# Both recurrent mixers of a streaming encoder layer on full 128x128 products, with the sample's tokens in a zero-padded third chunk

## The chip, the core and the metric

The program runs on one core of one Trainium2 chip. The metric is the device time of one execution in microseconds (us). The core has a tensor engine (PE; its weight loads are shown apart as PEld), a vector engine (DVE), a scalar engine (ACT), GpSimd (POOL) and a sequencer that issues most transfers (SP).

## What is computed

One layer of an encoder is applied to 256 prompt tokens and, with a state of its own, to 32 sample tokens. All tensors are float32. Cut to what matters here:

```python
h = rms_norm(x) * (1 + scale1) + shift1          # shift, scale, gate = silu(c) @ w_mod + b_mod
P = h @ w_in                                     # 2048 -> 14864 columns, for all branches and gates
# branch A: 8 heads, state 128x128:  S_t = diag(f_t) S_{t-1} + (1 - f_t) i_t^T,  o_t = q_t S_t
# branch B: 16 heads of 64, state 64x128: h_t = exp(dt_t a) h_{t-1} + dt_t x_t B_t^T,  y_t = h_t C_t
# branch C: v' = tril(W_s) v in chunks of 128 positions, y_c = u * (v' + b)
merged = sum(sigmoid(g_k) * (y_k @ w_branch_k) for k in (A, B, C))
x = x + gate1 * (merged @ w_out)
x = x + gate2 * (relu(h2 @ w_up) ** 2 @ w_down)  # 2048 -> 8192 -> 2048
```

The outputs are x of both sequences after a last norm, and the new states of both.

## The kernel before

Activations stand feature-major: 128 features on the partitions, and 288 token columns, of which 0 to 127 and 128 to 255 are the prompt's two chunks and 256 to 287 the sample. A weight tile of 128x1024 comes from HBM (SP's queue), is split by ACT into a rounded half `whi` (L395) and by DVE into the rest `wlo` (L396), and is used in three products per 128x128 block: `whi`*`lo`, `whi`*`hi`, `wlo`*`hi` (L413 to L415, first products L382 to L384). There are some 13,600 of these, and they are called streamed products below. Each has its own weight load.

Around them lies the work of the branches, in float32, where a product is two PE instructions (two passes) and a transpose is one:

- `load_x`, `transpose_x` (L171, L181): x comes token-major and is transposed block by block, at the start and again for the residual before the output projection. The sample's 32 tokens are a third, 32-row transpose of each of the 16 blocks (tile `xs`).
- `mixer_a` (L558), one head a call: decays within a chunk by levels L = 1, 2, 4 ... 128. For each level the operands `z` are made (DVE L571, L572, L574, L575, ACT L573), then multiplied in 32x32 squares (L584, 9 of them) or larger ones (L601), and joined under a mask (DVE L586, L589). The levels follow each other. Then come k to token-major (`to_tokens`, L534), the states (L620) and the outputs (L631, L633).
- `do_dt` (L726) and `mixer_b` (L801), two heads a call: x to token-major (L817), states (L827), and for each of the two heads the decay rows (L847), their exponential and mask (L850 to L854), and the products with x, 64 output rows each (L856). exp(a) for the carried state is brought to 64 rows per head by small products (`pair_rows`, L701, L704).
- `mixer_c`, `finish_c` (L960, L983): the products within chunks (L987).
- the modulation `silu(c) @ w_mod`: part on PE with 32 output rows (L246, L298), part summed on DVE (L274), some of it with every few weight tiles.

In each of these the sample is a chunk of 32 tokens: products whose contraction has 32 rows, beside the prompt's with 128. The profile writes a product's weights as rows*columns: `128*128` is the whole array, `128*32`, `128*64`, `32*128`, `32*64` and `16*64` are parts of it.

The order on each engine is not written out. A scheduler places the instructions by a simulated timeline and priorities: weight tiles and their split have the highest (`PRIO`), results of streamed products the next, and the mixers are put between streamed products where their operands are ready. Each engine then runs its own list strictly in order. Two PSUM buffers (`aux`) serve all the small products.

Of the kernel before, what the change touches and what calls it, by code (L numbers as in the profile page):

```python
# [36 lines left out]
def tile_step(ctx, tc, io, outs):  # L37
# [22 lines left out]
    # column pairs by which a branch's gates run ahead of its outputs  # L60
# [4 lines left out]
    def nm(s):  # L65
        uid[0] += 1
        return f"{s}_{uid[0]}"

# [37 lines left out]
    # triangular mask [s, t]: 1 where s <= t  # L106
# [3 lines left out]
    # scan resets at the chunk starts  # L110
# [4 lines left out]
    # selector that adds the four column groups of the modulation products  # L115
# [4 lines left out]

    lv_masks = {}
# [17 lines left out]
        # its 32-blocks next to each other  # L139
# [22 lines left out]
    # ones in one column of a sequence  # L162
# [5 lines left out]
    # x token-major, three blocks at a time (the sample's two)  # L168
    xrow = {}

    def load_x(engines, small):  # L171
# [5 lines left out]
        for i in range(8):  # L177
            xrow[2, i] = small("xs", 2 * P)[0:DEC]
            G.dma_start(out=xrow[2, i], in_=io["x_sample"][0, :, i * 2 * P:(i + 1) * 2 * P])

    def transpose_x(j):  # L181
        ps = aux()
        for c, (t0, n) in enumerate(CH):
            i, k = divmod(j, 2 if c == 2 else 3)
# [1070 lines left out]
```

## Time and profile before

| | us |
|---|---|
| median of 3 runs (lowest, highest) | 2113.21 (2109.93, 2116.8) |
| the profiled execution: span (the page gives no other time of it) | 2112.9 |
| DVE busy, ACT busy, POOL busy | 1442.7, 985.7, 156.6 |
| HBM read | 405 MB, 194 GB/s over the span |

Mean granted TensorE clock: 0.996 of 2.4 GHz. The page's busy time of PE counts matmuls that overlap in the pipeline, so a stretch of PE's timeline is read by the distance between the starts of its instructions. Stages of the program by the trace: the norm and the products that don't need the whole modulation to about 311 us, branch C to 380, branch A to 757, branch B to 1045, branch B's merge to 1160, output projection to 1269, the MLP to the end.

### The profile page before, as it was taken

The page shows a single profiled execution, that of the slowest core. Times are in us where ns is not written, and L with a number is a line of the kernel's source. Part 1 is how long each engine was busy: PE and PEld are TensorE (multiplying, and loading weights), DVE is VectorE, ACT ScalarE, POOL GpSimd, SP SyncE. Part 2 cuts the span into 40 slices and gives each one's busy share as a digit, 9 for nine tenths or more (in the row PEclk, how much of TensorE's full clock was granted, in tenths as well). Part 3 has the DMA queues.
Part 4 walks back from the last instruction along what each step waited for, and adds up shares of the span by engine and source line. Part 5 has one row for each costly group of instructions (what it writes and reads, how often), then busy time and mean ns, then how long its engine had stood idle before and what let it go on. Part 6 is the DMA issues. An engine that isn't in the chain of part 4 may idle for free.

```text
span 2112.9 us, 40517 instructions
## 1 busy us (share of the span) xinstructions
PE 2079.8 (98%) x16336; PEld 1966.6 (93%) x16336; DVE 1442.7 (68%) x2546; ACT 985.7 (47%) x1553; POOL 156.6 (7%) x278
## 2 busy tenths in 40 slices
PE   6999999999999999999999999999999999999997
PEld 4777998988999999999999999999999999999997
DVE  2565666756578887787988998766774455555565
ACT  4432584655555545545444445433453344334443
POOL 2020112000000110110100110000000000000010
PEclk9999999999999999999999999999999999999999
DMA  9987655456566565666877777666664555555542
GB/s 295 295 263 238 217 150 163 144 183 179 181 204 196 172 192 183 191 183 182 268 245 221 221 226 229 201 206 203 199 210 160 169 160 166 164 169 161 167 156 91
DMA packets 364844, 412.31 MB, mean 195 GB/s; under 512 B 14777, under 2 KB 325457, under 8 KB 364657
## 3 DMA queue, kind: packets, MB, share of 16 engines
q1 hardware_dynamic: 360784, 403.97, 61.3%
q0 software_dynamic: 3008, 4.58, 0.7%
q8 instruction: 128, 2.10, 0.4%
q10 hardware_dynamic: 864, 1.18, 0.2%
q14 instruction: 60, 0.48, 0.1%
HBM read 405.04 MB, written 4.62 MB: 194 GB/s over the span
## 4 chain that ended last, share of the span: by engine, by line
PE 96%; DVE 1%; ACT 1%; DMA 1%; POOL 0%; issue 0%; SPq 0%; POOLq 0%; ACTq 0%; DVEq 0%
PE mm L413 26%; PE mm L415 26%; PE mm L414 26%; PE mm L382 3%; PE mm L383 3%; PE mm L384 3%; PE modps L246 2%; PE modps L298 1%; PE aux L185 1%; PE aux L856 1%; PE aux L584 1%; PE modps L317 0%; PE aux L538 0%; PE modps L328 0%; PE aux L631 0%; PE aux L601 0%
## 5 line engine op out<-in xcount | busy, mean ns | idle before, releaser
L395 ACT CAST whi<-raw 128x1024 fp32r<-128x1024 f32 x568 | 595.4, 1049 | 911.3 <-PE mm L414 701.5
L396 DVE TENSOR_TENSOR wlo<-raw,whi 128x1024 fp32r<-128x1024 f32 x568 | 695.0, 1224 | 453.8 <-ACT whi L395 451.2
L413 PE MATMUL mm<-hlo,whi 128*128 128x288 f32 x1408 | 421.3, 300 | 0.0
L414 PE MATMUL mm<-hhi,whi 128*128 128x288 f32 x1408 | 419.2, 299 | 0.0
L415 PE MATMUL mm<-hhi,wlo 128*128 128x288 f32 x1408 | 413.2, 299 | 0.0
L414 PE MATMUL mm<-h2hi,whi 128*128 128x290 f32 x1024 | 303.9, 297 | 0.0
L413 PE MATMUL mm<-h2lo,whi 128*128 128x290 f32 x1024 | 303.5, 297 | 0.0
L415 PE MATMUL mm<-uhi,wlo 128*128 128x288 f32 x1024 | 303.3, 296 | 0.0
L415 PE MATMUL mm<-h2hi,wlo 128*128 128x290 f32 x1024 | 302.8, 297 | 0.0
L413 PE MATMUL mm<-ulo,whi 128*128 128x288 f32 x1024 | 301.2, 294 | 0.0
L414 PE MATMUL mm<-uhi,whi 128*128 128x288 f32 x1024 | 301.1, 294 | 0.0
L274 DVE SCALAR_TENSOR_TENSOR macc<-mraw,cT,macc 128x512 f32<-128x512 f32 x360 | 259.2, 745 | 24.5 <-DMA mraw<-in_w_mod_dram 24.2
L413 PEld LDWEIGHTS mm<-hlo,whi 128*128 128x128 f32 x1408 | 265.5, 189 | 9.1 <-issue 6.8
L414 PEld LDWEIGHTS mm<-hhi,whi 128*128 128x128 f32 x1408 | 265.8, 189 | 2.4 <-issue 0.9
L415 PEld LDWEIGHTS mm<-hhi,wlo 128*128 128x128 f32 x1408 | 263.3, 189 | 3.3 <-issue 1.0
L413 PEld LDWEIGHTS mm<-h2lo,whi 128*128 128x128 f32 x1024 | 194.0, 189 | 0.5 <-ACT r L1162 0.2
L415 PEld LDWEIGHTS mm<-h2hi,wlo 128*128 128x128 f32 x1024 | 193.9, 190 | 0.2 <-issue 0.2
L414 PEld LDWEIGHTS mm<-h2hi,whi 128*128 128x128 f32 x1024 | 193.9, 189 | 0.1
L413 PEld LDWEIGHTS mm<-ulo,whi 128*128 128x128 f32 x1024 | 193.0, 188 | 0.4 <-issue 0.4
L414 PEld LDWEIGHTS mm<-uhi,whi 128*128 128x128 f32 x1024 | 192.6, 188 | 0.0
L415 PEld LDWEIGHTS mm<-uhi,wlo 128*128 128x128 f32 x1024 | 192.2, 188 | 0.1
L382 PE MATMUL mm<-hlo,whi 128*128 128x288 f32 x448 | 138.6, 309 | 0.4 <-DVE hlo L472 0.4
(398 smaller groups left out, 3085.4 us busy)
## 6 DMA issues: line engine op xcount, KB each, us to landing
raw<-in_w_in_dram SPq DMA_DIRECT2D x204, 512.0 KB, 3.9
mraw<-in_w_mod_dram SPq DMA_DIRECT2D x128, 512.0 KB, 4.1
raw<-in_w_up_dram SPq DMA_DIRECT2D x128, 512.0 KB, 3.8
raw<-in_w_down_dram SPq DMA_DIRECT2D x128, 512.0 KB, 3.4
raw<-in_w_mod_dram SPq DMA_DIRECT2D x64, 512.0 KB, 5.0
raw<-in_w_branch_dram SPq DMA_DIRECT2D x48, 512.0 KB, 4.2
raw<-in_w_out_dram SPq DMA_DIRECT2D x32, 512.0 KB, 4.6
raw<-in_w_in_dram SPq DMA_DIRECT2D x56, 256.0 KB, 4.7
```

The source lines that it names most:

```text
L185: TE.transpose(ps[:, t0:t0 + n], xrow[c, i][:, k * P:(k + 1) * P], ident[0:n, 0:n])
L246: TE.matmul(ps[32 * cg:32 * cg + 32, 0:w], cT[:, k, :], raw[:, i, :], start=k < 4, stop=k >= 12)
L274: V.scalar_tensor_tensor(out=acc[s], in0=raw[:, i], scalar=cs, in1=acc[s], op0=ALU.mult, op1=ALU.add)
L298: TE.matmul(ps[32 * cg:32 * cg + 32, 0:256], cT[:, k, :], raw[:, cg * 256:(cg + 1) * 256], start=k == 0, stop=k == NB - 1)
L382: TE.matmul(pt, whi[:, i, cs], alo[k], start=i == 0, stop=False)
L383: TE.matmul(pt, whi[:, i, cs], ahi[k], start=False, stop=False)
L384: TE.matmul(pt, wlo[:, i, cs], ahi[k], start=False, stop=i == nk - 1)
L395: S.copy(out=whi, in_=raw)
L396: V.tensor_sub(out=wlo, in0=raw, in1=whi)
L413: TE.matmul(pts[b], whi[:, i, cs], alo[k], start=k == 0, stop=False)
L414: TE.matmul(pts[b], whi[:, i, cs], ahi[k], start=False, stop=False)
L415: TE.matmul(pts[b], wlo[:, i, cs], ahi[k], start=False, stop=k == nk - 1)
```

## The change

Lists of products can be issued together: `together` issues the first and puts the others right behind it on PE. The sample is the last 32 rows of a third chunk that covers tokens 160 to 287 (`C3`, `LAST`); where the other 96 rows must not count, one operand is a buffer that is zero there (`pads`, `mpads`, `wsTs`). x of the sample is loaded as four blocks on the four groups of 32 partitions, and transposed four blocks at once. In `mixer_a` the operands of levels 1 to 8 are made first, then all their products are issued together, then the same for levels 16 to 128. In `mixer_b` the products of both heads are issued together, alternating between the two halves of the columns, and exp(a) is read from the decay rows by ACT instead of `pair_rows`. The reads of `ssm_d` come by transfers in place of `pair_rows`.

```diff
+C3 = ((0, 128), (128, 128), (160, 128))
+LAST = slice(96, 128)
+    def together(works):
+        first = works[0]()
+        with tc.issue_after(first.ins), tc.high_priority(offset=PRIO):
+            for work in works[1:]:
+                work()
+    pads = [const.tile([P, P], F32, name=f"pad{i}") for i in range(2)]
+    mpads = [const.tile([P, 2, DEC], F32, name=f"mpad{i}") for i in range(2)]
+    for t in pads + mpads:
+        G.memset(t, 0.0)
 def load_x
-        for i in range(8):
-            xrow[2, i] = small("xs", 2 * P)[0:DEC]
-            G.dma_start(out=xrow[2, i], in_=io["x_sample"][0, :, i * 2 * P:(i + 1) * 2 * P])
+        for i in range(2):
+            xrow[2, i] = small("xs", 2 * P)
+            for q in range(4):
+                G.dma_start(out=xrow[2, i][32 * q:32 * q + DEC].rearrange("p (c f) -> p c f", f=P),
+                            in_=xsv[:, 2 * i:2 * i + 2, q])
+    def transpose_xs():
+        ps = aux()
+        for c in range(4):
+            i, k = divmod(c, 2)
+            TE.transpose(ps[:, c * P:(c + 1) * P], xrow[2, i][:, k * P:(k + 1) * P], ident)
+        return ps
 def to_tokens
-        for c, (t0, n) in enumerate(CH):
-            TE.transpose(pt[0:n, c * P:(c + 1) * P], src[:, t0:t0 + n], ident)
-        S.copy(out=dst[:, 0:2], in_=pt[:, 0:2 * P].rearrange("p (c f) -> p c f", c=2))
-        V.tensor_copy(out=dst[0:DEC, 2], in_=pt[0:DEC, 2 * P:3 * P])
+        for c, (t0, n) in enumerate(C3):
+            TE.transpose(pt[:, c * P:(c + 1) * P], src[:, t0:t0 + n], ident)
+        nc_ = 3 if pad is None else 2
+        S.copy(out=dst[:, 0:nc_], in_=pt[:, 0:nc_ * P].rearrange("p (c f) -> p c f", c=nc_))
+        if pad is not None:
+            V.tensor_copy(out=pad[LAST], in_=pt[LAST, 2 * P:3 * P])
 def mixer_a
-        for L in (1, 2, 4, 8, 16, 32, 64, 128):
...
+        for levels in ((1, 2, 4, 8), (16, 32, 64, 128)):
+            zs = {L: level_operands(L, q, k, b) for L in levels}
             pa = aux()
+            together([w for i in reversed(range(4)) for w in level_products(levels[i], pa[:, 96 * i:], *zs[levels[i]])])
+            for i, L in enumerate(levels):
+                level_pairs(L, pa[:, 96 * i:], att, atc)
...
-        for c, (t0, n) in enumerate(CH):
-            TE.matmul(pst[:, c * P:(c + 1) * P], kt[0:n, c], vA[h][0:n, c], start=True, stop=True)
+        for c in range(3):
+            TE.matmul(pst[:, c * P:(c + 1) * P], kt[:, c] if c < 2 else kts, vA[h][:, c], start=True, stop=True)
...
-            TE.matmul(po[:, t0:t0 + n], vA[h][0:n, c], att[0:n, t0:t0 + n], start=True, stop=c == 0)
+            TE.matmul(po[:, t0:t0 + n], vA[h][:, c], att[:, t0:t0 + n], start=True, stop=c == 0)
 def mixer_b
-        py = aux()
+        ms, e2, mm = mpads[j % 2], tt("e2"), []
         for a in range(2):
...
+            S.activation(out=e2[a * BP:(a + 1) * BP, 0:160], in_=pa[a * BP:(a + 1) * BP, 128:T], func=AF.Exp)
...
-            for c, (t0, n) in enumerate(CH):
-                TE.matmul(py[a * BP:(a + 1) * BP, t0:t0 + n], xdt[0:n, c, a * BP:(a + 1) * BP], m[0:n, t0:t0 + n],
-                          start=True, stop=True)
+        py = aux()
+        together([partial(TE.matmul, py[a * BP:(a + 1) * BP, t0:t0 + n], xdt[:, c, a * BP:(a + 1) * BP],
+                          mm[a][:, t0:t0 + n] if c < 2 else ms[:, a], start=True, stop=True)
+                  for c, (t0, n) in reversed(list(enumerate(CH))) for a in range(2)])
         po = aux()
...
-        pair_rows(po[:, 160:320], j, ea[:, 128:T])
-        e2 = tt("e2")
-        S.copy(out=e2[:, 0:160], in_=po[:, 160:320])
```

`level_operands`, `level_products` and `level_pairs` are the three parts of the old loop over levels, with the same instructions, but that the sample's square stands on rows and columns 96 to 127. The same replacement of a 32-row chunk by `C3` is made in `mixer_b_cb`, `finish_c`, `do_dt`, the states of `mixer_b` (`xds` in a zero-padded buffer) and the statistics of x.

How the order moves, on PE, at two places. In the rows, `aux` is the small products' PSUM buffer, `z` a level's operands, `mm` a streamed product's PSUM buffer.

PE in `mixer_a`, second head, before (left out: streamed and modulation products):

```order
L584 MATMUL aux_5353<-z_5347 32x32 x9
L584 MATMUL aux_5371<-z_5365 32x32 x9
...
L584 MATMUL aux_5389<-z_5383 32x32 x9
L584 MATMUL aux_5407<-z_5401 32x32 x9
...
L584 MATMUL aux_5425<-z_5419 32x32 x9
L601 MATMUL aux_5448<-z_5442 32x32 x2
...
L601 MATMUL aux_5461<-z_5455 64x64
L601 MATMUL aux_5448<-z_5442 32x32 x2
L601 MATMUL aux_5461<-z_5455 64x64
```

The same head in the change:

```order
L75 MATMUL aux_5293<-z_5287 32x32
L78 MATMUL aux_5293<-z_5287 32x32 x8
L78 MATMUL aux_5293<-z_5281 32x32 x9
L78 MATMUL aux_5293<-z_5275 32x32 x9
L78 MATMUL aux_5293<-qA_4958,kA_4672 32x32 x9
...
L75 MATMUL aux_5362<-z_5356 64x64
L78 MATMUL aux_5362<-z_5356 64x64
L78 MATMUL aux_5362<-z_5350 32x32 x4
L78 MATMUL aux_5362<-z_5344 32x32 x9
L78 MATMUL aux_5362<-z_5338 32x32 x9
```

Level 1 of this head (`qA`, `kA`) stood apart too, so five stretches between streamed products have become two; over all heads 47 have become 15.

PE in `mixer_b`, first call, before, behind the states:

```order
L847 MATMUL aux_8717<-ac_3246,sel_3247 128x288
...
L856 MATMUL aux_8716<-m_8719,xdt_8689 64x128 x2
L856 MATMUL aux_8716<-m_8719,xdt_8689 64x32
L847 MATMUL aux_8730<-ac_3246,sel_3247 128x288
...
L859 MATMUL aux_8743<-xbc_2991,stB_8691 128x128
L860 MATMUL aux_8743<-xbc_2991,snT_8686 128x32
L704 MATMUL aux_8743<-eacum,ident 64x160 x2
...
L856 MATMUL aux_8716<-m_8732,xdt_8689 64x128 x2
L856 MATMUL aux_8716<-m_8732,xdt_8689 64x32
```

and in the change:

```order
L900 MATMUL aux_8622<-ac_3218,sel_3219 128x288
...
L900 MATMUL aux_8631<-ac_3218,sel_3219 128x288
...
L75 MATMUL aux_8642<-mpad_107,xdt_8595 64x32
L78 MATMUL aux_8642<-mpad_107,xdt_8595 64x32
L78 MATMUL aux_8642<-m_8624,xdt_8595 64x128
L78 MATMUL aux_8642<-m_8633,xdt_8595 64x128
L78 MATMUL aux_8642<-m_8624,xdt_8595 64x128
L78 MATMUL aux_8642<-m_8633,xdt_8595 64x128
L918 MATMUL aux_8649<-xbc_2964,stB_8597 128x128
L919 MATMUL aux_8649<-xbc_2964,snT_8592 128x32
```

The two heads' products are one stretch, the products with the carried state follow it directly, and those of `pair_rows` are gone.

## Rows read from the trace of the kernel before

**Rows 1.** The page: an engine's busy time, share and instructions; the chain's shares.
```profile
PE 2079.8 (98%) x16336; PEld 1966.6 (93%) x16336; DVE 1442.7 (68%) x2546; ACT 985.7 (47%) x1553; POOL 156.6 (7%) x278
PE 96%; DVE 1%; ACT 1%; DMA 1%; POOL 0%; issue 0%; SPq 0%; POOLq 0%; ACTq 0%; DVEq 0%
```
**Rows 2.** PE's timeline, branch A: start us, us, engine, line, operation, out<-in, shape, count.
```profile
485.11 0.29 PE L413 MATMUL mm<-hlo,whi 128*128 128x288 f32 x1
...
487.77 0.29 PE L415 MATMUL mm<-hhi,wlo 128*128 128x288 f32 x1
```
**Rows 3.** PE's timeline: one level's products of `mixer_a`.
```profile
417.26 0.30 PE L414 MATMUL mm<-hhi,whi 128*128 128x288 f32 x1
417.49 0.38 PE L584 MATMUL aux<-qA,kA 128*32 128x32 f32 x18
417.80 0.40 PE L415 MATMUL mm<-hhi,wlo 128*128 128x288 f32 x1
418.03 0.29 PE L413 MATMUL mm<-hlo,whi 128*128 128x288 f32 x1
```
**Rows 4.** PE's timeline: two levels' products that follow each other.
```profile
480.21 0.30 PE L413 MATMUL mm<-ylo,whi 128*128 128x288 f32 x1
480.43 0.57 PE L584 MATMUL aux<-z 128*32 128x32 f32 x36
...
481.17 0.29 PE L415 MATMUL mm<-yhi,wlo 128*128 128x288 f32 x1
```
**Rows 5.** PE's timeline: one head's products of `mixer_b`, of three chunks.
```profile
784.64 0.29 PE L414 MATMUL mm<-hhi,whi 128*128 128x288 f32 x1
784.86 0.88 PE L856 MATMUL aux<-m,xdt 128*64 128x128 f32 x6
...
785.91 0.30 PE L413 MATMUL mm<-hlo,whi 128*128 128x288 f32 x1
```
**Rows 6.** PE's timeline: `mixer_b`, carried state and `pair_rows`.
```profile
783.14 0.38 PE L859 MATMUL aux<-xbc,stB 128*128 128x128 f32 x2
783.36 0.31 PE L860 MATMUL aux<-xbc,snT 128*128 128x32 f32 x2
783.59 0.49 PE L704 MATMUL aux<-eacum,ident 16*64 16x160 f32 x4
...
784.25 0.29 PE L414 MATMUL mm<-hhi,whi 128*128 128x288 f32 x1
```
**Rows 7.** PE's timeline: the states of `mixer_b`, two chunks of 128 rows, one of 32.
```profile
860.97 1.02 PE L827 MATMUL aux<-xdd,btk 128*128 128x128 f32 x6
...
862.17 0.29 PE L415 MATMUL mm<-hhi,wlo 128*128 128x288 f32 x1
```
**Rows 8.** PE's timeline, output projection: x of two blocks transposed.
```profile
1184.36 0.38 PE L185 MATMUL aux<-ident,xt 128*128 128x128 f32 x2
1184.67 0.24 PE L185 MATMUL aux<-ident,xs 32*128 32x32 f32 x1
...
1185.63 0.30 PE L414 MATMUL mm<-mhi,whi 128*128 128x288 f32 x1
```
**Rows 9.** PE's timeline: three transposes of `to_tokens`.
```profile
492.13 0.49 PE L538 MATMUL aux<-ident,kd 128*128 128x128 f32 x3
...
492.59 0.29 PE L415 MATMUL mm<-hhi,wlo 128*128 128x288 f32 x1
```
**Rows 10.** Stretches: us, PE, PEld, DVE, ACT, POOL busy, clock, DMA share, GB/s.
```profile
0.00:180.00 180.00, 164.08 (x1169) 119.57 (x1170) 94.31 (x207) 71.49 (x146) 27.60 (x67) 1.00 0.88 280
1185.00:1210.00 25.00, 25.00 (x186) 24.38 (x186) 25.00 (x47) 12.34 (x23) 6.80 (x4) 1.00 0.76 233
```
**Rows 11.** What PE waited for: us in total, times, longest us.
```profile
PE aux L584 <- DVE atc L589: 0.6, 1, 0.6
```
**Rows 12.** Groups by line, ACT: busy us, mean ns, idle before and releaser.
```profile
L900 ACT ACT_TABLE_LOAD x15 | 19.2, 1283 | 2.3 <-PE mm L415 2.1
```

More of the change, by code (lines that the diff above doesn't have):

```diff
@@ L1 @@
 from contextlib import ExitStack
+from functools import partial
 from itertools import chain
@@ L119, in tile_step @@
         V.tensor_add(out=selm, in0=selm, in1=ident[:, 32 * q:32 * q + 2])
+    sel4 = const.tile([P, DEC], F32, name="sel4")
+    V.tensor_reduce(out=sel4, in_=ident.rearrange("p (q t) -> p t q", q=4), axis=mybir.AxisListType.X, op=ALU.add)
+    pads = [const.tile([P, P], F32, name=f"pad{i}") for i in range(2)]
+    mpads = [const.tile([P, 2, DEC], F32, name=f"mpad{i}") for i in range(2)]
+    for t in pads + mpads:
+        G.memset(t, 0.0)
     lv_masks = {}
@@ new lines, in level_products @@
+    def level_products(L, pa, zl, zr):
+        works = []
+        if L <= 32:
+            for t0 in range(0, T, 32):
+                c, g = divmod(t0 // 32, 4) if t0 < SEQ else (2, 3)
+                works.append(partial(TE.matmul, pa[32 * g:32 * g + 32, 32 * c:32 * c + 32], zl[:, t0:t0 + 32],
+                                     zr[:, t0:t0 + 32], start=True, stop=True))
+            return works
+        hf = L // 2
+        for s0 in range(0, P, L):
+            for c, (t0, _) in enumerate(CH[:2]):
+                works.append(partial(TE.matmul, pa[s0:s0 + hf, c * hf:(c + 1) * hf], zl[:, t0 + s0:t0 + s0 + hf],
+                                     zr[:, t0 + s0 + hf:t0 + s0 + L], start=True, stop=True))
+        return works
@@ new lines, in level_pairs @@
+    def level_pairs(L, pa, att, atc):
+        if L <= 32:
+            mk = lv_masks[L]
+            V.copy_predicated(out=atc[:, 0:64].rearrange("p (c t) -> p c t", t=32),
+                              mask=mk.unsqueeze(1).to_broadcast([P, 2, 32]),
+                              data=pa[:, 0:64].rearrange("p (c t) -> p c t", t=32))
+            V.copy_predicated(out=atc[LAST, 64:96], mask=mk[LAST], data=pa[LAST, 64:96])
+            if L == 32:
+                for g in range(4):
+                    src = atc[32 * g:32 * g + 32, 0:64].rearrange("p (c t) -> p c t", t=32)
+                    G.tensor_copy(out=att[32 * g:32 * g + 32, 0:SEQ].rearrange("p (c t) -> p c t", t=P)
+                                  [:, :, 32 * g:32 * g + 32], in_=src)
+                G.tensor_copy(out=att[LAST, SEQ:T], in_=atc[LAST, 64:96])
+            return
+        hf = L // 2
+        for s0 in range(0, P, L):
+            rows = slice(s0, s0 + hf)
+            V.tensor_copy(out=att[rows, 0:SEQ].rearrange("p (c t) -> p c t", t=P)[:, :, s0 + hf:s0 + L],
+                          in_=pa[rows, 0:L].rearrange("p (c t) -> p c t", t=hf))
@@ L699, in evac_z @@
         S.activation(out=zB[j], in_=ps, func=AF.Silu)
-    def pair_rows(out, j, rows):
-        for a in range(2):
-            TE.matmul(out[a * BP:(a + 1) * BP], ident[0:BH, 2 * j + a:2 * j + a + 1].to_broadcast([BH, BP]), rows,
-                      start=True, stop=True)
     dtc = mconst.tile([BH, 4], F32, name="dtc")
@@ L714, in setup_dt @@
             G.dma_start(out=dtc[:, 1:2], in_=io["ssm_a_log"].rearrange("o h -> h o"))
-            G.dma_start(out=dtc[:, 2:3], in_=io["ssm_d"].rearrange("o h -> h o"))
+            for a in range(2):
+                G.dma_start(out=dcol[a * BP:(a + 1) * BP],
+                            in_=io["ssm_d"].rearrange("o (j a) -> a (o j)", a=2)[a].partition_broadcast(BP))
         S.activation(out=dtc[:, 3:4], in_=dtc[:, 1:2], func=AF.Exp)
         V.tensor_scalar_mul(out=dtc[:, 3:4], in0=dtc[:, 3:4], scalar1=-1.0)
-        ps = aux()
-        for j in range(BH // 2):
-            pair_rows(ps[:, j:j + 1], j, dtc[:, 2:3])
-        V.tensor_copy(out=dcol, in_=ps[:, 0:BH // 2])
     dts = {}
@@ L790, in mixer_b_cb @@
         pc = aux()
-        for c, (t0, n) in enumerate(CH):
-            TE.matmul(pc[0:n, t0:t0 + n], Bf[:, t0:t0 + n], Cf[:, t0:t0 + n], start=True, stop=True)
+        for (t0, n), (s0, _) in zip(CH, C3):
+            TE.matmul(pc[:, t0:t0 + n], Bf[:, s0:s0 + P], Cf[:, t0:t0 + n], start=True, stop=True)
         cb = cbB[g] = bt("cb")
@@ L1097, in evac_out @@
             (V if j > NB - 4 else G).tensor_add(out=rst[:, 0:T], in0=rst[:, 0:T], in1=sq)
+    ps = transpose_xs()
+    xsT = [tt("xsT", 8 * DEC) for _ in range(2)]
+    for i in range(2):
+        S.copy(out=xsT[i], in_=ps[:, i * 8 * DEC:(i + 1) * 8 * DEC])
     wv_out = io["w_out"][0].rearrange("(k p) n -> p k n", p=P)
@@ L1102, in tile_step @@
             x1.append(ht("x1", F32)[:, 0:T])
-            S.copy(out=x1[i], in_=transpose_x(i)[:, 0:T])
+            S.copy(out=x1[i][:, 0:SEQ], in_=transpose_x(i)[:, 0:SEQ])
         product_group(wv_out, j * P, NB, mhi, mlo, each(evac_out), j)
```

166 lines of the change are left out of this document (79 added, 87 removed).

## Prediction, made before the changed kernel was run

> **What bounds the kernel.** I read the page first, then the chain, PE's waits, and PE's timeline at each place that the change touches. PE is busy 98% of the span, and the chain that ended last runs through PE for 96% of it [rows 1]. So a microsecond that PE no longer spends is worth nearly a microsecond, wherever the other engines have slack, and the rest is a question of what PE spends. Busy time doesn't tell that, since matmuls overlap; starts do. In [rows 2] the two streamed products are 20 products apart and start 2.66 us apart: 0.133 us each. That is the pace of a PE that changes nothing from one product to the next.
>
> An excursion to a small product is read against it: from the start of the first instruction of other shape, or the streamed product before it, to the second streamed product behind it, less 0.133 us for each streamed product in between. One level of `mixer_a` (18 instructions) costs 418.03 - 417.26 - 0.27 = 0.50 us [rows 3]. Of this 0.10 is the way in (0.23 from the last streamed product to the first small one, not 0.133), and 0.10 is lost behind it, where the first streamed product takes 0.23. Two levels in one stretch (36 instructions) cost 481.17 - 480.21 - 0.27 = 0.69 us [rows 4]. So the second level's 18 instructions added only 0.19 us, 0.011 each: most of the 0.50 is the change of shape, not the work.
>
> **The change, part by part, in PE time.**
>
> 1. Gathered levels. Stretches of level products fall from 47 to 15 (counted in both orders). A stretch that joins another saves 0.50 - 0.19 = 0.31 us [rows 3, 4], and 32 do: **-9.9 us**. The products themselves stay.
> The Trainium skill, "TensorE: Matmul & The Clock Gate", section "Wait — 56ns, not 53.3ns?", speaks against this term: start to start of matmuls never falls below about 25 ns, however small they are. By it 18 more instructions would add 0.45 us, a joined stretch would save 0.05, and the term would be 1.6 us. By it the time would be 2087 us. The trace disagrees, at 0.011 us each [rows 4], so this gets no chance of its own, and the term stands.
>
> 2. `mixer_b`'s products with x. A head's stretch costs 785.91 - 784.64 - 0.27 = 1.00 us [rows 5], and there are 16: 16.0 us. Now there are 8, for two heads each, all of one shape. No row shows such a stretch. At worst the two halves of the columns run one after the other: 2 x 1.00, less 0.31 for the excursion saved, less 0.30 per head for the change of shape at the 32-row chunk (part 4), 1.09 us. At best they run beside each other: one head's time without that change, 0.70 us. `pair_rows` is the nearest row: its four instructions of 160 columns, two on each half, are through in 784.25 - 783.59 - 0.23 = 0.43 us [rows 6] (0.23 for the first streamed product behind, as in [rows 3]); four in a row would need 4 x 160/128 x 0.11 = 0.55, 0.11 us being what 128 columns take in the same rows (783.36 - 783.14, two instructions). I take 0.85 us: 8 x 0.85 = 6.8, **-9.2 us** (-7.3 to -10.4).
>
> 3. `pair_rows` in `mixer_b` goes, and the two products with the carried state now follow those of part 2 without an excursion of their own. The four kinds together cost 784.25 - 783.14 - 0.13 = 0.98 us [rows 6]. What stays is 783.59 - 783.14 = 0.45. Saved 0.53 x 8 = 4.2. Against it, the second decay product (L847), which shared its excursion with L856, stands alone: 8 x 0.10. **-3.4 us.** ACT's read of the decay rows replaces a copy, off the path.
>
> 4. The 32-row third chunk. Two products of 128 rows (four instructions) and one of 32 rows (two) cost 862.17 - 860.97 - 0.13 = 1.07 us [rows 7]. A full 128-column instruction is (783.36 - 783.14) / 2 = 0.11 us [rows 6], so six are 0.66, with 0.11 lost behind them 0.77: padding to full size saves 0.30, since the extra rows cost nothing and two changes of shape go. This form stands 32 times: states and outputs of `mixer_a` (8 + 8), states of `mixer_b` (8), branch C's products (8). **-9.6 us** (outputs and branch C have narrower last products than [rows 7] and might save 0.2 or 0.4: -6.4 to -12).
>
> 5. Sample x in the output projection. Two blocks, with two 32-row transposes, cost 1185.63 - 1184.36 - 0.13 = 1.14 us [rows 8]. Three equal transposes cost 492.59 - 492.13 - 0.13 = 0.33 [rows 9], four about 0.44. Saved 0.70 x 8 = 5.6, less 0.44 for the sample's own four: 5.2. But DVE is busy 25.00 of 25.00 us here [rows 10], on modulation sums and weight rests, and nothing takes that work away; PE would come to wait for `wlo`. I count half: **-2.6 us** (0 to -5.2).
>
> 6. The start. The same 16 transposes and the setup's `pair_rows` go (5.2 and some 1.5 us by the prices above), but the order now breaks the modulation's products into 46 stretches instead of 35: +11 x 0.31 = 3.4. That leaves 3.3, in a stage with the transfers at 0.88 of all engines' time and PE at 164 of 180 us [rows 10], where PE often waits for weights. **-1.5 us** (0 to -3.3).
>
> What is free: ACT gets nine more table loads (counted in the orders) of 1.28 us [rows 12], 11.5 us, hidden by ACT's idle half [rows 1]; a load that falls between a weight tile's arrival and its cast delays that tile, but three split tiles are held ahead, at 24 products of 0.133 us each almost 10 us of PE work. DVE loses 31 of 2,548 instructions. The POOL queue has as many x loads as before, two more for `ssm_d` and five more memsets early, and nobody on PE's path waits for these last.
>
> New waits: a gathered stretch can't begin before its last level is ready, and PE runs in order, so everything behind it waits too. PE has one such wait now, 0.6 us [rows 11]. With 24 gathered stretches (16 in `mixer_a`, 8 in `mixer_b`) I allow 0.1 us each: +2.4.
>
> Sum: -9.9 - 9.2 - 3.4 - 9.6 - 2.6 - 1.5 + 2.4 = **-33.8 us**, against the profiled execution's 2112.9, which is 0.3 us under the median of the runs, so the same holds for that: 2079 us, 1.6% faster. A measurement of this kernel tells some 0.3%, 6 us, from no change.
>
> **Rivals.**
>
> *DVE takes over as the bound.* It is full in the output projection [rows 10], and a shorter PE stage in branch B brings it nearer there as well, with the modulation's sums tied to the weight tiles. Then parts 5 and 6 give nothing and parts 2 and 3 half: -9.9 - 6.3 - 9.6 + 2.4 = -23.4, 2090 us. For it: the 25 of 25. Against: over the whole run DVE has a third of its time free, and PE kept its pace even in that stretch.
>
> *The change of shape is not what is saved.* The small products use the time in which the next weights are loaded, and PE loses elsewhere what it gains here; or the scheduler's new order spends it on more breaks, as it already does in the modulation. Then the gain is within 6 us: about 2109 us. Against: [rows 3, 4] are the same products with and without the break, next to the same streamed products.
>
> *Slower: the gathered stretches starve PE.* Place: the 16 `together` of `mixer_a`, where 16 DVE operations and four exponentials must be done before the first product, on a DVE that also splits the weights, and the 8 of `mixer_b`, which now wait for both heads. If PE stood there on average longer than 36.2 / 24 = 1.5 us, the gain is gone; at 2 us the time is 2112.9 - 36.2 + 48 = 2125. For it: the one wait of the kind that the trace has [rows 11] is for just such a mask. Against: the scheduler puts streamed products between the two stretches of a head, and issues the last-made level first, so that the others are ready.
>
> **Chances and range.** Forecast (a gain of 27 to 47 us): 0.70. DVE as the bound (14 to 27 us): 0.17. No gain: 0.07. Starved: 0.06. Faster by over 0.3%: 0.87; within 0.3%: 0.07; slower: 0.06. The low end takes the good ends of parts 2, 4, 5 and 6 (1.2 + 2.4 + 2.6 + 1.8) and no new waits (2.4): -44, 2069; the high end goes past the first rival to about -14, 2099. That leaves the last two rivals and a little more out.
>
> **What would show it.** In the changed profile: two stretches of level products a head, of 72 and 48 instructions, the first about 1.1 us; `mixer_b`'s x products in one stretch of 12 instructions and about 0.85 us; the six-instruction states at 0.77 us by the same reading; no 32-row weights in the mixers; PE's mean pace of 0.133 us unchanged; the gain lying between 360 and 1045 us of the old span, with only a few microseconds before and after. It is wrong if PE's list of waits shows level operands, masks or `wlo` with more than some 10 us in all, or if the stretches have those lengths and the branch stages are still as long as before.

## The result, and the profile after

The changed kernel takes **2087.16 us** (median of four runs, 2083.99 to 2088.53), against 2112.71 for the kernel before on the same chip: ratio 0.9878, 95% interval 0.9863 to 0.9893, or 25.6 us less. The range (2069 to 2099) holds it, and faster was right; of the 33.8 us that were forecast three quarters came. The profiled execution took 2083.99 us with a span of 2082.3, so it is 3.2 us under the median. The profile before stands above its own: its span is 2112.9 us, and the times of the changed kernel's runs are 1.7 us over their spans. So the differences between the two profiles (30.6 us in the spans) come out 5 us larger than those of the medians.

Where the time went is read from PE's timeline in both traces: the start of the first product with each operand divides the span into stages.

| stage, us | before | changed | difference | forecast |
|---|---|---|---|---|
| start, to the first product of `hlo` | 34.8 | 41.8 | **+7.0** | -1.5 (both rows) |
| to branch C's first product (`sumC`) | 276.5 | 276.4 | -0.1 | |
| branch C, to the first product of `qA` | 68.2 | 64.9 | -3.3 | -2.4 (8 of part 4's 32) |
| branches A and B, merges, to the first product of `mlo` | 780.9 | 750.9 | **-30.0** | -27.3 (the rest of 1 to 4, waits) |
| output projection, to the first product of `h2lo` | 108.2 | 104.1 | -4.1 | -2.6 |
| MLP, to PE's last product | 833.8 | 833.8 | 0.0 | 0 |

The boundary between the third and fourth rows is not the same event in both kernels: in the change `qA`'s products come last in the gathered stretch. So only the sum of the two rows, -33.3, can be set against the forecast of -29.7. Some 1.5 us of it (an estimate from experiment 6's stretches at half clock) is no gain of the change: in the profile before, the granted clock stands at 0.50 (1.2 GHz) from 328.8 to 332.2 and from 362.9 to 366.3 us, in the changed one only from 335.2 to 338.6, each time behind a wait of PE. So the mixers gave about 2 us more than forecast, and the start, which was to give 1.5 us, took 7.0.

The same reading, added up over all stretches of small products from `sumC` to `mlo` (start of the streamed product before to start of the second one behind, less 0.133 us for each streamed product, less PE's waits), gives 142.6 us before and 106.2 in the change: 36 us less (up to 1.5 of it by the clock), for the 32.1 of parts 1 to 4. The stretches with level products fall by about 12 of these, those of `mixer_b` with `xdt`, the carried state and `pair_rows` by about 13.

**The mixers.** PE's timeline of the changed kernel, in three places (columns as in [rows 2]). First one head's levels 1 to 8, 72 instructions in one stretch, which answers to [rows 3, 4]:

```profile
650.25 0.29 PE L444 MATMUL mm<-hhi,whi 128*128 128x288 f32 x1
650.48 0.22 PE L75 MATMUL aux<-z 128*32 128x32 f32 x1
...
651.37 0.40 PE L445 MATMUL mm<-hhi,wlo 128*128 128x288 f32 x1
651.61 0.30 PE L443 MATMUL mm<-hlo,whi 128*128 128x288 f32 x1
```

From the first small product to the streamed one behind it pass 651.37 - 650.48 = 0.89 us, 0.012 for each of the 72, and the stretch costs 651.61 - 650.25 - 0.27 = 1.09, the "about 1.1" of the prediction. The pace of 0.011 that [rows 4] showed nearly holds for twice as many. Levels 16 to 128 cost 1.19 by the same reading.

Then `mixer_b`'s products with x, both heads, with the two carried-state products behind them ([rows 5, 6]):

```profile
958.66 0.30 PE L444 MATMUL mm<-hhi,whi 128*128 128x288 f32 x1
958.89 0.24 PE L75 MATMUL aux<-mpad,xdt 128*64 128x32 f32 x1
...
959.03 0.64 PE L78 MATMUL aux<-m,xdt 128*64 128x128 f32 x8
959.60 0.49 PE L918 MATMUL aux<-xbc,stB 128*128 128x128 f32 x2
...
960.07 0.38 PE L445 MATMUL mm<-hhi,wlo 128*128 128x288 f32 x1
960.28 0.30 PE L443 MATMUL mm<-hlo,whi 128*128 128x288 f32 x1
```

Together 960.28 - 958.66 - 0.27 = 1.35 us. Of that 0.45 is the price of the two carried-state products, so the twelve with x cost 0.90 (0.85 was taken). And the states of `mixer_b`, all six instructions 128 rows deep ([rows 7]):

```profile
869.59 0.61 PE L879 MATMUL aux<-xdd,btk 128*128 128x128 f32 x4
870.03 0.39 PE L879 MATMUL aux<-pad,btk 128*128 128x128 f32 x2
870.17 0.38 PE L445 MATMUL mm<-hhi,wlo 128*128 128x288 f32 x1
870.39 0.29 PE L443 MATMUL mm<-hlo,whi 128*128 128x288 f32 x1
```

870.39 - 869.59 - 0.13 = 0.67, where 0.77 was worked out and [rows 7] had 1.07.

**The start.** PE's timeline of the changed kernel (in brackets the idle time before an instruction, and what ended it), and what its DMA engines did from 17 to 31 us (busy tenths and GB/s in 40 equal slices of 0.35 us, then a queue's packets and an issue's median time to landing):

```profile
34.10 1.08 PE L277 MATMUL modps<-raw,cT 128*32 128x256 f32 x8 [6.77 <-DMA raw<-in_w_mod_dram]
...
41.80 0.61 PE L412 MATMUL mm<-hlo,whi 128*128 128x288 f32 x1
```
```profile
DMA  9999999999999999993700129999899900000112
GB/s 351 369 302 366 287 348 348 278 322 339 433 369 311 357 351 342 345 149 33 38 18 12 35 82 124 88 89 50 0 21 27 25 23 23 26 23 18 32 67 99
...
q0 software_dynamic: 356, 0.55, 58.6%
...
dcol<-in_ssm_d_dram POOLq DMA_DIRECT2D x2, 2.0 KB, 11.2
```

From 23.3 us on, 15 of the 22 slices show under 40 GB/s instead of 350; GpSimd's queue (q0) holds 58.6% of the engines' time with 0.55 MB. The two transfers of `dcol` (L770) are under way then: 8 values of `ssm_d` to each of 64 partitions, every second one of the source, 1,024 values in all. In the trace's packet records they are 32 packets of 128 bytes, which took 3.1 us each in the median, 5.2 at most, where a packet of 4,096 bytes of the same queue took 0.18. They start between 23.0 and 28.2 us, the last ends at 33.4, and up to 15 are under way at a time. (The view puts a packet's whole time and bytes into the slice in which it starts, so its busy tenths fall to 0 while these packets still run.) PE waits 6.8 us behind them for a tile of `w_mod`.

### The profile page after: what moved, and what is told of

It reads as the page before. It is cut to its first block, busy times and chain, and to the rows that moved or that the text cites. A ratio compares the mean times of both kernels' runs of the same rounds, so it can differ in the third digit from the quotient of the medians.

```text
span 2082.3 us, 40240 instructions
## 1 busy us (share of the span) xinstructions
PE 2034.7 (98%) x16248; PEld 1941.9 (93%) x16248; DVE 1453.9 (70%) x2515; ACT 998.1 (48%) x1553; POOL 155.7 (7%) x284
## 4 chain that ended last, share of the span: by engine, by line
PE 60%; ACT 0%; DVE 0%; issue 0%; ACTq 0%
PE mm L445 20%; PE mm L443 20%; PE mm L444 20%; PE aux L1208 0%; PE aux L208 0%; ACT stage L1282 0%; PE aux L879 0%; PE modps L75 0%; PE modps L78 0%; PE aux L78 0%; PE aux L918 0%; PE aux L867 0%; PE aux L75 0%; PE aux L900 0%; PE pr L1265 0%; DVE x L1246 0%
```

## The experiments

Unless it says otherwise, a difference is one of medians. The kernel before took 2110.5 to 2112.7 us beside these versions, on several chips, so medians alone don't tell differences of under some 2 us. What is in brackets behind a time is its ratio to the kernel before, with the 95% interval.

**1. `ssm_d` as a row.** In the changed kernel:

```diff
-            for a in range(2):
-                G.dma_start(out=dcol[a * BP:(a + 1) * BP],
-                            in_=io["ssm_d"].rearrange("o (j a) -> a (o j)", a=2)[a].partition_broadcast(BP))
+            G.dma_start(out=drow, in_=io["ssm_d"][0].partition_broadcast(P))
+        for a in range(2):
+            V.tensor_copy(out=dcol[a * BP:(a + 1) * BP],
+                          in_=drow[a * BP:(a + 1) * BP].rearrange("p (j a) -> p a j", a=2)[:, a])
```

> Edit: in the changed kernel ssm_d is read once, as a row of 16 values to each of the 128 partitions (one piece of 64 bytes a partition), and two VectorE copies sort it into dcol; everything else stays. Theory A (the two transfers of ssm_d, 1,024 single values of 4 bytes, hold the DMA engines from 21 to 29 us, where they moved some 25 GB/s while 99% busy): PE's wait for w_mod falls from 14.6 us to about 6, the first hlo product starts near 35 us and not 41.8, and the time falls by some 6 to 8 us, to 2079 to 2081 us; nothing behind the start changes. Rival B (the start is late because the sample's x comes in pieces of 512 bytes, or because of the broken order of the modulation's products): the first hlo product stays at 40 to 42 us, and the time at 2086 to 2089.

Measured: 2076.86 us (0.9836, 0.982 to 0.9853), 10.3 less than the changed kernel. The first `hlo` product starts at 33.6 us. From 17 to 31 us no slice shows less than 282 GB/s. PE's waits (engine, operand and line, what it waited for: us in total, times, longest), first of the changed kernel and then of this one, the rows for `w_mod`:

```profile
PE modps L277 <- DMA raw<-in_w_mod_dram: 14.6, 7, 6.8
```
```profile
PE modps L277 <- DMA raw<-in_w_mod_dram: 7.5, 8, 4.0
```

Theory A holds for the start, where the profiles differ by 8.2 us; the time is 2 us under its range. Of the 2.2 us of the spans that lie behind the start, 1.5 are in branch C, where this profile lacks the changed kernel's stretch at half clock. By the stages above this version stands at -1.2 for the start and -31.4 for branches A and B against the kernel before.

**2. The scattered transfers in the kernel before.** The reverse: lines L715 and L718 to L721 of the kernel before give way to the two transfers of the changed one.

> Edit: in the kernel before, ssm_d is read by the two scattered transfers of the changed kernel, and the setup's products of pair_rows for it go (some 1.5 us of PE); nothing else changes. Theory A (the transfers hold the DMA engines): the first hlo product starts near 41 us and not 34.8, the time rises by 5 to 8 us to 2118 to 2121 us, and the DMA queues show 5 us or more at under 50 GB/s. Rival B (other causes for the late start): 2111 to 2113 us, first hlo product at 33 to 35 us.

Measured: 2119.39 us (1.0038, 1.0024 to 1.0052), 7.2 more than the kernel before on the same chip. The first `hlo` product starts at 43.7 us. Its waits in the first 50 us, and the rate from 17 to 33 us (40 slices of 0.4 us):

```profile
PE modps L246 <- DMA raw<-in_w_mod_dram: 12.2, 5, 7.7
```
```profile
GB/s 371 397 366 410 379 399 241 177 210 323 371 387 354 215 52 19 26 38 31 59 26 54 34 95 49 44 19 1 0 1 16 33 51 97 138 161 184 192 236 264
```

The transfers alone, without anything else of the change, make the hole of some 7 us. With 1 and 2 the late start has its cause.

**3. The levels one after the other.**

```diff
-        for levels in ((1, 2, 4, 8), (16, 32, 64, 128)):
-            zs = {L: level_operands(L, q, k, b) for L in levels}
+        for L in (1, 2, 4, 8, 16, 32, 64, 128):
+            zl, zr = level_operands(L, q, k, b)
             pa = aux()
-            together([w for i in reversed(range(4)) for w in level_products(levels[i], pa[:, 96 * i:], *zs[levels[i]])])
-            for i, L in enumerate(levels):
-                level_pairs(L, pa[:, 96 * i:], att, atc)
+            for work in level_products(L, pa, zl, zr):
+                work()
+            level_pairs(L, pa, att, atc)
```

> Edit: in the changed kernel mixer_a takes its eight levels one after the other again, operands, products and joining of each, with nothing issued together; its order has 44 stretches of level products in place of 15. Theory A (a change of shape is what is saved, 0.31 us a stretch): 29 x 0.31 = 9.0 us more, less the waits of the gathered stretches in the changed profile (2.7 us for one), so +6 to +9: 2093 to 2096 us, all of it in branch A. Rival B (PE loses elsewhere what the gathering gains): within 2 us of the changed kernel, 2085 to 2089. Rival C (the gathering starves PE): faster than the changed kernel.

Measured: 2089.21 us, only 2.1 over the changed kernel, and the intervals against the kernel before overlap (0.988 to 0.9909 here). By the profiles the stretch from `sumC` to `mlo` is 819.5 us for 815.8, +3.7. So theory A's 6 to 9 did not come, and by the time alone rival B (within 2 us) can't be told from this. The waits say where the rest is. PE's list from 355 us to the first `mlo` product, of the changed kernel and then of this one:

```profile
PE aux L75 <- ACT vA L580: 2.7, 1, 2.7
PE aux L75 <- DVE mpad L911: 2.1, 1, 2.1
PE modps L329 <- DMA mraw<-in_w_mod_dram: 1.3, 1, 1.3
PE aux L578 <- ACT iv L586: 1.0, 1, 1.0
PE aux L693 <- DVE stA L682: 1.0, 1, 1.0
PE aux L578 <- DVE atc L640: 0.9, 2, 0.5
...
```
```profile
PE aux L578 <- ACT vA L580: 2.9, 1, 2.9
PE aux L663 <- DVE atc L640: 0.8, 1, 0.8
...
```

9.2 us against 4.1, with one row of 0.2 and two of 0.2 that are left out. Each of the two profiles has one stretch of 3.4 us at half clock between `sumC` and `mlo` (at 335 us in the changed kernel, at 460 us here), so the clock isn't the difference. Without its waits PE's work is 3.7 + 5.1 = 8.8 us longer with the levels apart, which is 29 stretches at 0.30: the price was right, and more than half of the gain went into waits. What the gathering is worth in time, 2.1 us by the medians and 3.7 by the stage, is not clear of the noise. I had subtracted 2.7 for waits, and that very wait, for `vA`, is there without the gathering too.

**4. The 32-row chunk back.** In the four products `kt`/`kts` (L679), `vA`/`att` (L691), `btk`/`xds` (L879) and `vt`/`wsTs` (L1048), the third chunk's operands are cut to rows 96 to 127, as here:

```diff
-            TE.matmul(pn[:, c * P:(c + 1) * P], btk[:, c], xdd[:, c] if c < 2 else xds, start=True, stop=True)
+            TE.matmul(pn[:, c * P:(c + 1) * P], btk[:, c] if c < 2 else btk[LAST, c],
+                      xdd[:, c] if c < 2 else xds[LAST], start=True, stop=True)
```

> Edit: in the changed kernel the sample's products contract over rows 96 to 127 alone in four places (states and outputs of mixer_a, states of mixer_b, branch C's products), 32 in all; loads, padding buffers and everything else stay. Theory A (a change of shape at the short chunk costs 0.30 us by the kernel before; 0.30 to 0.39 by the difference of the two profiles' states and outputs): +9.6 to +12 us, 2096 to 2099 us, spread over branches C, A and B. Rival B (the 32-row shape costs nothing, and the gain came from the order): 2085 to 2089.

Measured: 2093.71 us (0.9918, 0.9903 to 0.9933), +6.5; by the profiles +8.5 from `sumC` to `mlo`. PE's timeline, states of `mixer_b`:

```profile
876.14 0.61 PE L879 MATMUL aux<-xdd,btk 128*128 128x128 f32 x4
876.68 0.48 PE L879 MATMUL aux<-pad,btk 32*128 32x128 f32 x2
877.09 0.40 PE L445 MATMUL mm<-hhi,wlo 128*128 128x288 f32 x1
877.33 0.29 PE L443 MATMUL mm<-hlo,whi 128*128 128x288 f32 x1
```

877.33 - 876.14 - 0.13 = 1.06 for 0.67: with the same loads, buffers and order, contracting over fewer rows costs 0.39 us more. Theory A in the mechanism; the total is 3 us below its range. By the lists of waits from 355 us on PE waits 7.5 us here for 9.2 in the changed kernel, so its work is 8.5 + 1.7 = 10.2 us longer, for 32 places.

**5 and 6. `mixer_b`'s two heads.** Both in the version of experiment 1. First, still one stretch, but head after head:

```diff
-                  for c, (t0, n) in reversed(list(enumerate(CH))) for a in range(2)])
+                  for a in range(2) for c, (t0, n) in reversed(list(enumerate(CH)))])
```

> Edit: in the version with ssm_d as a row (2076.9 us), mixer_b's twelve instructions of a pair of heads stay one stretch, but in another order: all six of the first head (one half of the columns), then the six of the second. Theory A (the two halves run beside each other when they alternate): the stretch with the two products behind it, 1.35 us now, becomes 1.6 to 1.85, +2 to +4 us in all, 2079 to 2081. Rival B (the order doesn't matter, the hardware overlaps or serialises both alike): 1.30 to 1.40 us, time within 1 us of 2076.9 but for the spread of single runs (3 us).

Second, each head's six products issued as soon as they are ready: `together`, and exp and mask of the sample (`ms`), move into the loop over heads.

> Edit: in the version with ssm_d as a row, mixer_b's products with x are issued per head again, each as soon as its own decays are ready (six instructions each, of one shape), so 16 stretches for 8; exp and mask of the sample's decays are also per head. Theory A (joining two heads saves a change of shape and lets the halves run side by side): a head's stretch takes 0.70 us, two 1.40, where the joined one takes 0.90: +0.5 x 8 = 4 us, less the one wait on the joined operands (2.1 us for mpad): +2 to +4, 2079 to 2081 us. Rival B (the joined stretch only moves the wait): within 1 us of 2076.9, or faster.

Measured: in turn 2077.49 us (one run); apart 2080.54 (0.9859, 0.9846 to 0.9873), +3.7. PE's timeline in turn, and then one head alone in the version apart:

```profile
976.74 0.29 PE L444 MATMUL mm<-hhi,whi 128*128 128x288 f32 x1
976.97 0.30 PE L75 MATMUL aux<-mpad,xdt 128*64 128x32 f32 x2
...
977.81 0.49 PE L920 MATMUL aux<-xbc,stB 128*128 128x128 f32 x2
```
```profile
987.99 0.29 PE L443 MATMUL mm<-hlo,whi 128*128 128x288 f32 x1
988.21 0.30 PE L75 MATMUL aux<-mpad,xdt 128*64 128x32 f32 x2
988.35 0.63 PE L78 MATMUL aux<-m,xdt 128*64 128x128 f32 x4
988.90 0.40 PE L444 MATMUL mm<-hhi,whi 128*128 128x288 f32 x1
```

From the streamed product before to the first start behind: one head 988.90 - 987.99 = 0.91 us, two heads alternating 959.60 - 958.66 = 0.94 (above), two in turn 977.81 - 976.74 = 1.07. So the second head's six instructions cost 0.03 us when they alternate between the halves of the columns, and 0.16 in turn: the halves do run beside each other, and even in turn mostly so, less than theory A of that run wanted. From `sumC` to `mlo` the version apart takes 4.7 us longer than experiment 1's, with no stretch at half clock in either profile; the intervals of the two medians just overlap. A head alone costs 0.89 and not the 0.70 that I had taken for its best case.

The run in turn showed something else. Its branches A and B took 753.4 us for 749.5 in the version of experiment 1, and 8 x 0.13 explains 1.0 of it. Stretches of that profile, and then the same two of experiment 1's (columns as in [rows 10]; PEclk is the seventh value after the window, behind POOL):

```profile
451.20:454.60 3.40, 3.40 (x57) 2.94 (x56) 3.15 (x11) 0.34 (x2) 0.00 (x0) 0.50 0.42 134
...
802.80:806.20 3.40, 3.40 (x16) 3.38 (x16) 3.37 (x6) 0.00 (x0) 0.00 (x0) 0.50 0.17 57
```
```profile
451.20:454.60 3.40, 3.40 (x64) 2.56 (x62) 3.12 (x12) 0.71 (x2) 0.00 (x0) 1.00 0.45 139
...
802.80:806.20 3.40, 3.40 (x27) 3.40 (x27) 3.37 (x9) 1.05 (x1) 0.00 (x0) 1.00 0.62 205
```

Both profiles have the waits of 2.7 us for `vA` and 2.1 for `mpad` just before. In one of them the granted clock then stood at 0.50 (1.2 GHz) twice, in the other at 1.00. In the second of these stretches PE started 16 products at half clock and 27 at full: 11 x 0.133 = 1.5 us. Two stretches of that length would make the other 2.9 (an estimate, as the first holds small products too). So a wait of over 2 us in the mixers is followed, in some profiles, by a loss of another 1.5 us.

**7. The sample's x in the output projection, block by block.** In the version of experiment 1, `load_x` and `transpose_x` take the old 32-row form there, and the start keeps the new one.

> Edit: in the version with ssm_d as a row, the output projection takes the sample's x as 16 transposes of 32 rows again, one with each block; the start keeps its four full transposes. Theory A (each such transpose costs PE 0.35 us, and PE bounds the stage in spite of the full VectorE): the stage from the first mlo to the first h2lo product goes from 103.9 to 108 us, the time to 2081 us. Rival B (VectorE bounds the stage): the stage changes by under 1.5 us, and PE's list of waits shows wlo there in the version that has less PE work. Rival C (half of each, as I had counted): +2.6.

Measured: 2082.35 us (0.9867, 0.9853 to 0.988), +5.5. The stage takes 109.0 us for 103.9, two blocks cost 1.13 (1.14 in [rows 8]), and no PE wait stands in it in either version. VectorE is full there in the changed kernel as before:

```profile
1160.00:1185.00 25.00, 25.00 (x193) 25.00 (x192) 25.00 (x46) 13.29 (x24) 6.02 (x4) 1.00 0.71 221
```

Rivals B and C fall: 25.00 of 25.00 busy on VectorE was not a bound in this stage, and the whole 5.1 us were PE's.

**8 to 12. The waits.** ScalarE's timeline of the changed kernel, before the product that waits 2.1 us for `mpad` (its exp is the last row):

```profile
805.04 1.28 ACT L908 ACT_TABLE_LOAD   x1
806.34 0.42 ACT L908 ACTIVATE m<-m 128x256 f32<-128x256 f32 x1
806.77 1.28 ACT L956 ACT_TABLE_LOAD   x1
808.07 0.41 ACT L956 ACTIVATE sg<-mm 128x288 f32<-128x288 f32 x1
808.50 1.28 ACT L907 ACT_TABLE_LOAD   x1
809.79 0.30 ACT L907 ACTIVATE e<-aux 64x160 f32<-64x160 f32 x1
810.11 0.25 ACT L910 ACTIVATE mpad<-mpad 32x64 f32<-32x64 f32 x1
```

Of 5.3 us, 3.8 are table loads, as a gate's sigmoid comes between two exps. The wait for `vA` stands behind the same alternation of tables. The product that waits there reads `z`, `q` and `k` and not `vA`; so it is probably held by the PSUM buffer that the copy to `vA` empties, one of the two `aux`. No run gave the small products a third. Four versions of experiment 1's kernel tried to move such work. The first (8): `vA`'s copy on VectorE, the sample's exp and mask with more priority.

```diff
-        S.copy(out=dst[:, 0:nc_], in_=pt[:, 0:nc_ * P].rearrange("p (c f) -> p c f", c=nc_))
+        (V.tensor_copy if pad is None else S.copy)(out=dst[:, 0:nc_], in_=...)
...
+        with tc.high_priority(offset=EVP):
             S.activation(out=ms[LAST], in_=ms[LAST], func=AF.Exp)
...
```

> Edit: in the version with ssm_d as a row, the copy of branch A's values to token-major (vA) moves from ScalarE to VectorE, and the sample's exp and mask in mixer_b get the priority of the results of streamed products. Theory A (PE's waits of 2.7 us for vA and 2.1 for mpad come from ScalarE, where table loads of 1.28 us stand between): both waits go, -3 to -5 us, 2072 to 2074. Rival B (the waits come from the gathering itself and move to the next late operand): PE's waits between 350 and 1130 us stay at 8 us or more, time 2075 to 2079.

Measured: 2075.52 us (0.9839, 0.9826 to 0.9853), the same as experiment 1 within the intervals. `vA` is gone from PE's list, but 2.1 us for a level's `z` and 2.5 for `mraw` stand in its place, and 1.7 for `mpad` have stayed: rival B, though the list has 7.4 us from 350 to 1130 us and not its 8.

The next three (9, 10, 11) make the sample's exp and mask per head, beside the prompt's; 10 also takes three of branch C's additions to `ssC` to VectorE, and 11 `vA`'s copy too.

```diff
-        S.activation(out=ms[LAST], in_=ms[LAST], func=AF.Exp)
-        V.tensor_tensor(out=ms[LAST], ...)
+            S.activation(out=ms[LAST, a], in_=ms[LAST, a], func=AF.Exp)
+            V.tensor_mul(out=ms[LAST, a], in0=ms[LAST, a], in1=cb[LAST, SEQ:T])
...
-                G.tensor_add(out=ss, in0=ss, in1=sq[:, 0:T])
+                (V if j > 4 else G).tensor_add(out=ss, in0=ss, in1=sq[:, 0:T])
```

> Edit: in the version with ssm_d as a row, exp and mask of the sample's decays in mixer_b are made per head, beside those of the prompt, while the twelve products stay one stretch. Theory A (the wait of 2.1 us for mpad comes from ScalarE, which loads other tables between the prompt's exp and the sample's): the wait goes, and with it the half clock that two other profiles show behind it for 3.4 us (1.7 us of work): -2 to -4 us, 2073 to 2075 us. Rival B (the joined stretch itself waits for its latest head): a wait of 1 us or more stays on m or mpad, 2076 to 2078.

> Edit: as ms_per_head, and in branch C the last three of the seven additions to the sum of squares (ssC) are on VectorE (0.4 us each) and not on GpSimd (1.8 us each). Theory A: PE's wait of 2.3 us for ssC, which the kernel before has too, goes, and the half clock behind it that four profiles show from 327 to 338 us: another -2 to -4 us, 2070 to 2073. Rival B: the wait is taken over by the reciprocal behind it (2 us on VectorE) or by another operand: within 1 us of ms_per_head.

> Edit: as ms_ss, and the copy of vA is on VectorE. Theory A (ScalarE's table loads stand between the transposes of the values and their copy): with 77 table loads for 88 in the order, PE's wait of 2.7 us for vA goes without another in its place: 2067 to 2071. Rival B (as in va_dve, the waits of branch A move to a level's operand z and to mraw): within 1 us of ms_ss or above it.

Measured: 2083.52 (0.987, 0.9856 to 0.9884), 2081.33 (0.9858, 0.9844 to 0.9872) and 2078.0 us (0.9845, 0.9828 to 0.9862). The first is slower than experiment 1 by 6.7, clear of the noise; the interval of the second overlaps experiment 1's by a little, that of the third by most. Neither theory had any of the three times. PE's timeline and one wait of the first:

```profile
903.36 0.29 PE L445 MATMUL mm<-hhi,wlo 128*128 128x288 f32 x1
903.58 0.30 PE L75 MATMUL aux<-mpad,xdt 128*64 128x32 f32 x2
903.81 0.40 PE L443 MATMUL mm<-hlo,whi 128*128 128x288 f32 x1
904.05 0.29 PE L444 MATMUL mm<-hhi,whi 128*128 128x288 f32 x1
```
```profile
PE aux L919 <- ACT e L909: 2.6, 2, 2.4
```

`together` ties the later products to the first one. The first is the first head's sample product, whose operand is now ready early. So it starts early and alone, the ten others come in a second stretch, and in seven of the eight calls the carried state in a third (in one it shares the first): 904.05 - 903.36 - 0.27 = 0.42, and 0.89 and 0.45, for 1.35, eight times. That is 3.3 us, and a wait for `e` has come on top. Of 10's edit the wait for `ssC` (2.3 us) did go.

The last (12) is 11 with the second head's sample products first:

```diff
-                  for c, (t0, n) in reversed(list(enumerate(CH))) for a in range(2)])
+                  for c, (t0, n) in reversed(list(enumerate(CH))) for a in (1, 0)])
```

> Edit: as ms_ss_va, but the second head's sample products, whose operand is made last, are issued first in mixer_b's joined stretch. In the order this makes 8 stretches with x of them again, where ms_per_head, ms_ss and ms_ss_va have 16 (the first head's two sample products stood alone, and the carried state's two), 261 breaks of the streamed products for 282, and 74 table loads. Theory A (those three lost 5 to 8 us in branch B to the split stretches and the wait for e, and the edits are good otherwise): 8 x (0.43 + 0.45 + 0.89 - 1.35) = 3.4 us and most of the 2.6 us for e come back against ms_ss_va: 2072 to 2074, 3 to 5 us under the version with ssm_d as a row. Rival B (the operands made per head cost ScalarE and VectorE more than the stretches): the wait for e or for wlo stays, 2076 to 2079.

Measured: **2073.29 us** (0.9822, 0.9809 to 0.9836), 4.7 less than 11, whose interval it still overlaps a little. The stretch is one again in all eight calls and costs 1.35 in seven (the eighth stands behind a wait and at half clock), and the wait for `e` is gone. Waits of 2.2 us for `mpad` and for `z` have stayed, and `wlo` stands in PE's list with 2.6, as rival B had it. So of theory A the stretches and `e` are shown, and not that the other edits are good. By the median this is the fastest version, 13.9 us under the changed kernel; its interval does not touch the changed kernel's, but does touch experiment 1's, whose profiled execution was the shorter one (span 2071.9 us for 2073.2).

## Why the prediction was right, and where its steps were off

- **What bounds, and the unit of account.** Right. Reading a stretch by its starts gave prices near what was measured: 1.09 for a stretch worked out at 1.07 (0.69 + 2 x 0.19), 0.90 for 0.85, 0.67 for 0.77. One step was loose: the sum was taken from the profile's span of 2112.9 us as if it were a time. By the 1.7 us between the two (above) that execution was above the median of the runs and not 0.3 under it; the gain of 33.8 doesn't hang on this.
- **Part 1, gathered levels (-9.9).** Right in PE's work, by experiment 3: 8.8 us for 29 stretches (about 12 for all 32 by the sum over stretches above). But 5.1 of the 8.8 were lost to waits, which the term did not see. The Trainium skill ("TensorE: Matmul & The Clock Gate", section "Wait — 56ns, not 53.3ns?") puts a floor of about 25 ns from start to start. The 72 instructions above disagree, at 0.012 us each (a product of two instructions takes 0.025, and in the second level of [rows 4] 0.19 / 9 = 0.021). That 2087 us, the time by that rule, is what was measured is a coincidence: the missing time lay in the start and in waits.
- **Parts 2 and 3, `mixer_b` (-9.2, -3.4).** Right in sum, about 13 us by the same sum. The twelve products cost 0.90, because the halves run beside each other (experiments 5 and 6). One reason was off: a head of one shape costs 0.89, not 0.70, so the change of shape is worth 0.11 there and not 0.30, while the second head costs 0.03. No run put `pair_rows` back in `mixer_b`: part 3 is read from the traces alone.
- **Part 4, the third chunk (-9.6).** Right by mechanism, 0.39 us in the states of `mixer_b`; 10.2 us of PE's work, 8.5 by the profiles and 6.5 by the medians of experiment 4.
- **Part 5, output projection (-2.6).** The term was halved for a full VectorE. That step was wrong: 4.1 us came, and taking the edit back cost 5.1 in the stage (experiment 7). VectorE was full in that stage, but nobody waited for it: PE's list had no `wlo` there.
- **Part 6, the start (-1.5), and "what is free".** The step that failed. Without the transfers of `ssm_d` PE gains 1.2 us to the first `hlo` product and 0.7 to branch C's first, of the 1.5 worked out. But I costed those transfers at nothing, since nobody on PE's path waits for them, and did not ask what the transfers of others would meet: they cost 7 to 10 us (medians of experiments 2 and 1; 8.2 us in the start by the profiles of 1). In the table the first two rows are 8.4 us worse than forecast and the others 5.1 better, so this is more than the whole miss.
- **New waits (+2.4).** Too small. From 355 us to the first `mlo` product PE waits 9.2 us in the changed profile and 3.8 before, and in other profiles some of the same waits are followed by half clock. Table loads, which I called hidden by ScalarE's idle half, stand ahead of the two longest. That they cause them is not shown: where experiments 8 to 12 moved that work, other waits came.
- **Rivals.** VectorE as the bound: refuted by experiment 7 for the output projection, though its 2090 lies near the result. No gain from fewer changes of shape: in time refuted by 4 (6.5 us, intervals apart); 3 refutes it in PE's work alone. Starved by the gathering: its mechanism is there, 5.1 us of 8.8 in experiment 3, and did not decide.

With the start right the forecast would have been met: experiment 1's version, 2076.9 us, is 2 us from 2079. That it comes so near is in part luck: the waits took 3 us more than allowed, and PE's work in the mixers and the output projection fell by more than forecast. What stays open is which single waits the gathering itself causes; only their sum was tried.

## What to carry to other kernels

Price small products by the distance of starts, the change of shape and the instructions apart; then gathering, padding to the full shape and using both halves of the columns can each be added up from rows. Set the waits against them: of the 8.8 us that gathering the levels took off PE's work, 5.1 came back as waits. When products are tied to one another, let the operand that is made last lead. And ask of every new transfer, however few its bytes and however late its reader, what its pieces look like and whose transfers stand behind it.

## What the runs showed of the hardware

- Packets of 128 bytes put together from single values of 4 bytes took 3.1 us each in the median, and 32 of them, up to 15 at a time, held nearly all traffic for 7 us. The Trainium skill ("DMA: Bandwidth & Descriptors", section "Why small descriptors are slow (HBM only)") says that each packet carries a fixed cost of a few cycles; the trace agrees that small pieces are dear, but the size here is of another order, and why is not shown.
- Two groups of six instructions on the two halves of the columns took 0.94 us when they alternated and 1.07 in turn, one group 0.91.
- A contraction over 32 rows, between products over 128, cost 0.39 us more than the same product over 128.
- After waits of 2.1 and 2.7 us in the middle of steady work the granted clock stood at 0.50 for 3.4 us in some profiles and at 1.00 in others of the same stretch of program.
